# Router preparation moved ahead of the output projection, zero matmuls in the router's waits, and the first gather in two parts

## The chip, the cores and the metric

The kernel runs on one core of one Trainium2 chip. The metric is device microseconds (us) of one execution, from the first instruction to the end; lower is better. Engines are named as the profile names them: PE is the matmul engine, PEld its weight loads, DVE, ACT and POOL the elementwise engines, SP the engine that issues most transfers. The trailing q in SPq, ACTq or PEq means the engine's sequencer.

## What is computed

A batch of 1 with 256 tokens of 1024 features goes through one mixer block and then two decoder layers, all in float32. Each decoder layer has an attention half (three branches, gates, an output projection) and an experts' half. The experts' half is what the change touches:

```python
x = x + (gate1[:, None, :] * (merged.astype(x.dtype) @ w_o)).astype(x.dtype)
h2 = modulate(rms_norm_2(x, norm2_g), shift2, scale2)
y_moe = hier_moe(h2, w_router_group, b_router_group, w_router_expert, b_router_expert,
                 w_exp_gate, w_exp_up, w_exp_down)
x = x + (gate2[:, None, :] * y_moe).astype(x.dtype)
```

`hier_moe` scores 4 groups of 8 experts each, picks one group and two of its experts for each token, and adds up the chosen experts' outputs, weighted by both softmaxes. All 32 experts of a layer have three matrices of 2 MB.

## The kernel before, in words

**Weights.** Every weight matrix comes in chunks of 2 MB (128 partitions x 4096 columns). Each of the 32 experts has three chunks, `weg` (gate), `weu` (up) and `wed` (down). SP issues their transfers (line 429). One large tile, `memory`, holds everything; the class `Plan` gives each small tile and each chunk its columns from a dry run. A second tile is called `parts` while it holds split operands, and `spare` in the experts' half, where it takes two chunks. A transfer waits until the last reader of its columns is done, so when memory is full the next chunk waits for an expert's chunk to be used up. Eleven of a layer's 96 expert chunks are under way or there before the first expert runs; the twelfth (expert 3's `wed`) takes the columns of expert 0's `weg`.

**End of the attention half** (`front`, lines 1264 to 1297). `ma` holds the merged branches, split in high and low parts by ACT (L1284) and DVE (L1285); just before, DVE adds the last branch with L1281 (times the gate tile `g1`) and L1282 (the sum), in four pairs of feature tiles. The output projection `tm_out` then runs 96 matmuls of 512 columns into the PSUM banks `po`. `add_x` (DVE L600, ACT L592) adds them to x and takes its squares.

**Start of the experts' half** (`moe`, line 1705). The router's weights `wr` come by a POOL-issued transfer (line 396). Eight matmuls `shift @ wr` of 36 columns make the bias `br`, and eight DVE operations (L1735) make `wg_` = gain x `wr`. Four zero matmuls open the accumulators `acc`. `flip` (L631) transposes x, sixteen router matmuls of 36 columns follow, then some forty small DVE operations (L1746 to L1772), and four matmuls that count each token's place within its expert. `group(0)` gathers the tokens of experts 0 to 3:

```python
self.mm(p[:, i, :], self.x[:, t, j + i::8], S[:, t].rearrange("p e s -> p (e s)"), t == 0, t == 1)
```

Its 16 matmuls have x as the stationary operand, every eighth column of it, and the one-hot matrix `S` of 4 x 32 places as the moving one. DVE (L1824) and ACT (L1822) write the results to `XG`, in turn. Then comes `overflow`, a branch for experts with over 32 tokens that all engines take part in (not taken in this execution), then the transposes of `back(0)` (L1835), then expert 0: 64 matmuls on `weg`, 64 on `weu`, and so on. `XG[:, j, s]` with `s` the expert's 32 places is all that an expert reads of the group.

All matmuls through the helper `mm` show as line 505. Float32 matmuls show as two records each in the trace, transposes as one. Tile's scheduler, not the source alone, sets each engine's order; each engine then runs its own list strictly in order.

Of the kernel before, what the change touches and what calls it, by code (L numbers as in the profile page):

```python
# [21 lines left out]
# ---------------------------------------------------------------- host layout  # L22
# [5 lines left out]
def _chunk(w):  # L28
    """[K*128, N] -> [128, K*N], row d = 128*k + p at partition p."""
    kp, n = w.shape  # L30
    return w.reshape(kp // 128, 128, n).transpose(1, 0, 2).reshape(128, -1)
# [160 lines left out]
# ---------------------------------------------------------------- the kernel  # L192
class Act:
    """Activations, features on partitions: float32 and its exact two-part split."""
# [5 lines left out]
class Dry:  # L200
    """Stands for anything in the run that only plans the memory."""
# [22 lines left out]
class Plan:  # L224
    """Sizes and lifetimes of all tiles by a dry run, and from them each tile's place and each weight chunk's time to
    start: as early as there is room for it. Times count the steps of the program that take or free memory."""
# [19 lines left out]
    def place(self, first):  # L246
        """An address for every tile, from the bottom, and for every chunk while it is used, from the top: the large
        and long ones first, and before them those that found no room."""
# [28 lines left out]
    def early(self):  # L277
        """Every chunk in turn starts as early as some place is free for it, in the main part or, while that is open
        for chunks, in the other."""
# [26 lines left out]
class Memory:  # L306
    """Columns of one tile, given out and taken back in the order of the program; the waits follow from the data."""
# [6 lines left out]
    def step(self):  # L314
        """One step on; the chunks whose time has come start."""
# [6 lines left out]
    def new(self, *sh, p=128, part=0):  # L322
        """A tile of this shape on the first p partitions."""
# [22 lines left out]
    def chunk(self):  # L346
        """The next weight chunk's number."""
        self.step()
        if self.tiles is None:
            self.plan.chunks.append([Plan.CHUNK, self.now, None, 0])  # L350
        self.got += 1
        return self.got - 1
# [6 lines left out]
    def turn(self, key, *sh, bufs=2, p=128, part=0):  # L359
        """One of bufs tiles of this shape, by turns, until done()."""  # L360
# [11 lines left out]
class Kernel:  # L372
# [26 lines left out]
    def order(self):  # L399
        """The weight chunks in the order in which they are used."""  # L400
# [19 lines left out]
    def start(self, n, t):  # L420
# [4 lines left out]
        # an expert half's last chunk in parts, so that little work is left after the last of them  # L425
# [6 lines left out]
    def get(self, *key, k=8, hold=False):  # L432
        """The next weight chunk; it is there until the next call, or until drop()."""
# [20 lines left out]
    def run(self, plan, dry):  # L454
# [24 lines left out]
        # the last norm: all but the last quarter times its gain before the rows' rs is there  # L479
# [7 lines left out]
    # -- helpers  # L487
    def turn_part(self, spare):
        """The second part of the memory is for split operands, or it is spare and takes weight chunks."""
# [14 lines left out]
    def mm(self, out, lhsT, rhs, start, stop):  # L504
        self.nc.tensor.matmul(out, lhsT=lhsT, rhs=rhs, start=start, stop=stop)  # L505

    def psb(self, tag="sm", name="pst"):
        """A bank of PSUM."""
        return self.ps.tile([128, 512], F, tag=tag, bufs=BANKS[tag], name=name)

    def split(self, f, n=4):
        """f = hi + lo, both exact in the tensor engine's one-pass float32."""
# [6 lines left out]
    def unit(self, src, a, n=1024):  # L519
        """The split of 1024 weights a partition."""  # L520
# [6 lines left out]
    def mm3(self, jobs, left):  # L527
        """out += w.T @ a, or a.T @ w, for every out, w, a, start, stop, from the parts: those with the weights' high
        part first. The product of both low parts is below float32's own rounding."""
# [6 lines left out]
    def fm_pair(self, w, act, m, K=8):  # L536
        """Feature tiles m, m+1 of the projection of act, features on partitions."""
# [10 lines left out]
    def tm(self, w, act):  # L548
        """The projection of act, tokens on partitions: two banks of 128 tokens."""
# [8 lines left out]
    def tm_out(self, w, act, accs, first, last):  # L558
        """accs[t][h] += the projection of four feature tiles of act."""
# [9 lines left out]
    def rsqrt(self, out, in_, scale, eps, tmp):  # L569
        """out = (in_*scale + eps) ** -0.5 on small tiles."""  # L570
# [3 lines left out]
    def newton(self, out, v):  # L574
        """out = v ** -0.5: a first guess from the bits, then three Newton steps; v is overwritten."""
# [11 lines left out]
    def squares(self, t, h):  # L587
        """The mean square of half a row of x, into ss."""
# [5 lines left out]
    def add_x(self, accs, last=False):  # L594
        """x += accs, and its mean squares."""
# [9 lines left out]
    def last_gain(self):  # L605
        """The last norm's gain on every partition."""
# [18 lines left out]
    def flip(self, v, by8, use):  # L625
        """Two feature tiles of v's transpose at a time: use(k, their bank)."""
# [7 lines left out]
    def norm_T(self, gain, shift=None):  # L634
        """The split of x's rms-norm, transposed: uT[d, t] * gain[d] (+ shift[d])."""
# [28 lines left out]
    def weave(chain, dense):  # L664
        """Trace the steps of a chain with pieces of dense work between them."""
# [4 lines left out]
    # -- block 1  # L670
    def block1(self):
# [10 lines left out]
        def softplus(out, x, t):  # L682
            """out = max(x, 0) + log1p(exp(-|x|)); t: four scratch tiles."""
# [15 lines left out]
        # forget gates and time steps, heads on partitions  # L699
# [19 lines left out]
        # token-major dt, exp(cumsum), decay to the chunk's end  # L719
# [14 lines left out]
        def conv(p, raw, out, j, wn, bn, nt):  # L734
            """causal conv of width 4 of psum tile p along time."""
# [73 lines left out]
        def gates():  # L809
            """The z gates of LRU and SSD; SSD's norm, features on partitions."""  # L810
# [83 lines left out]
        def ssd():  # L894
            # B.C scores, masked to s <= l
# [7 lines left out]
            # tokens on partitions: x*dt and x*d, B of chunk 0  # L903
# [1089 lines left out]
```

## Time and profile before

| | |
|---|---|
| median of 3 runs | 1986.38 us (1982.15 to 1988.5) |
| span of the profiled execution | 1985.8 us |
| PE, DVE, ACT busy | 84%, 48%, 28% of the span |
| DMA, mean over the span | 295 GB/s of at most about 430 |
| mean granted PE clock | 0.915 |

The profiled execution's own time is not among the three; its span is 0.6 us under their median. Shares over the whole span say little here: the span has stretches bound by PE (attention halves) and stretches bound by transfers (experts' halves), and each has to be read by itself.

### The profile page before, as it was taken

The page shows a single profiled execution, that of the slowest core. Times are in us where ns is not written, and L with a number is a line of the kernel's source. Part 1 is how long each engine was busy: PE and PEld are TensorE (multiplying, and loading weights), DVE is VectorE, ACT ScalarE, POOL GpSimd, SP SyncE. Part 2 cuts the span into 40 slices and gives each one's busy share as a digit, 9 for nine tenths or more (in the row PEclk, how much of TensorE's full clock was granted, in tenths as well). Part 3 has the DMA queues.
Part 4 walks back from the last instruction along what each step waited for, and adds up shares of the span by engine and source line. Part 5 has one row for each costly group of instructions (what it writes and reads, how often), then busy time and mean ns, then how long its engine had stood idle before and what let it go on. Part 6 is the DMA issues. An engine that isn't in the chain of part 4 may idle for free. (4 is left out here: it accounts for less than half of the span.)

```text
span 1985.8 us, 42525 instructions
## 1 busy us (share of the span) xinstructions
PE 1659.6 (84%) x18982; PEld 1379.8 (69%) x18982; DVE 958.3 (48%) x2013; ACT 557.6 (28%) x856; POOL 76.6 (4%) x54
## 2 busy tenths in 40 slices
PE   6999999999999887776677599999988877667774
PEld 6877669788988765555455398889987765545553
DVE  7896556788438433222222456784376332222222
ACT  6835444524425300000000235244253100000001
POOL 0001000000004000000000000000040000000000
PEclk9999999999989899888888799999998998788888
DMA  8654563563325799999999953642258999999996
GB/s 344 236 193 155 201 262 131 212 251 132 128 100 234 291 426 426 426 427 425 427 427 426 399 221 133 259 161 105 109 188 324 391 426 425 427 426 426 426 426 252
DMA packets 43119, 586.13 MB, mean 295 GB/s; under 512 B 4816, under 2 KB 5456, under 8 KB 7984
## 3 DMA queue, kind: packets, MB, share of 16 engines
q1 hardware_dynamic: 41904, 579.72, 71.6%
q0 software_dynamic: 1024, 3.61, 0.5%
q8 instruction: 151, 2.47, 0.5%
q14 instruction: 40, 0.33, 0.0%
HBM read 582.26 MB, written 1.05 MB: 294 GB/s over the span
## 5 line engine op out<-in xcount | busy, mean ns | idle before, releaser
L505 PE MATMUL pst<-parts 128*128 128x256 f32 (+2 forms) x4344 | 636.6, 306 | 17.1 <-DVE parts L523 12.4
L505 PEld LDWEIGHTS pst<-parts 128*128 128x128 f32 (+1 forms) x4344 | 578.7, 197 | 65.8 <-issue 17.7
L505 PE MATMUL pst<-memory 128*32 128x256 f32 (+11 forms) x5152 | 519.7, 354 | 83.6 <-DMA memory<-in_wed_dram 43.5
L505 PEld LDWEIGHTS pst<-memory 128*32 128x32 f32 (+5 forms) x5152 | 373.7, 157 | 189.2 <-issue 115.9
L505 PE MATMUL pst<-memory,spare 128*32 128x128 f32 (+1 forms) x6848 | 266.1, 317 | 136.1 <-DMA memory<-in_weu_dram 77.4
L523 DVE TENSOR_TENSOR parts<-memory,parts 128x1024 fp32r<-128x1024 f32 (+1 forms) x233 | 296.7, 1276 | 156.6 <-ACT parts L522 147.6
L522 ACT ACTIVATE parts<-memory 128x1024 fp32r<-128x1024 f32 (+1 forms) x233 | 245.6, 1057 | 425.0 <-PE pst L505 348.1
L505 PEld LDWEIGHTS pst<-memory,spare 128*32 128x32 f32 (+1 forms) x6848 | 237.4, 129 | 178.8 <-issue 117.7
L1886 DVE TENSOR_TENSOR spare<-pst,memory 32x256 f32<-32x256 f32 x256 | 107.6, 420 | 172.0 <-PE pst L505 169.1
L1870 ACT ACTIVATE memory<-pst 128x128 f32<-128x128 f32 x64 | 25.2, 393 | 544.7 <-PE pst L505 525.9
L1872 DVE TENSOR_TENSOR memory<-memory,pst 128x128 f32<-128x128 f32 x64 | 24.0, 375 | 193.8 <-PE pst L505 193.7
L1871 DVE TENSOR_TENSOR memory<-memory,pst 128x128 f32<-128x128 f32 x64 | 24.2, 378 | 193.3 <-ACT memory L1870 193.3
L505 PE MATMUL po<-parts 128*128 128x512 f32 x384 | 89.6, 392 | 2.0 <-ACT parts L515 1.5
L505 PEld LDWEIGHTS po<-parts 128*128 128x128 f32 x384 | 71.5, 188 | 20.6 <-ACT parts L515 3.0
L1822 ACT ACTIVATE spare<-pst,memory,gain 128x128 f32<-128x128 f32 x64 | 29.3, 457 | 189.0 <-DVE spare L1824 189.0
L505 PE MATMUL pst<-spare 128*32 128x128 f32 x1408 | 51.0, 304 | 25.9 <-DMA spare<-in_weu_dram 12.9
L505 PEld LDWEIGHTS pst<-spare 128*32 128x32 f32 x1408 | 45.4, 123 | 32.8 <-issue 26.2
L505 PE MATMUL acc<-spare,memory 128*128 128x512 f32 x128 | 59.8, 610 | 9.2 <-DVE spare L1886 9.2
L1824 DVE TENSOR_SCALAR spare<-pst,gain,memory 128x128 f32<-128x128 f32 x64 | 26.2, 409 | 66.1 <-PE pst L505 56.7
L1291 POOL TENSOR_TENSOR memory<-memory 128x1024 f32<-128x1024 f32 x16 | 47.8, 3019 | 209.8 <-ACT memory L1145 209.8
L505 PEld LDWEIGHTS acc<-spare,memory 128*128 128x128 f32 x128 | 21.8, 189 | 38.1 <-DVE spare L1886 22.8
L505 PE MATMUL pst<-spare,memory 128*32 128x256 f32 x352 | 27.4, 459 | 14.5 <-DMA spare<-in_wed_dram 8.5
(381 smaller groups left out, 974.1 us busy)
## 6 DMA issues: line engine op xcount, KB each, us to landing
memory<-in_weg_dram SPq DMA_DIRECT2D x54, 2048.0 KB, 39.1
memory<-in_weu_dram SPq DMA_DIRECT2D x52, 2048.0 KB, 39.3
memory<-in_wed_dram SPq DMA_DIRECT2D x52, 2048.0 KB, 39.1
memory<-in_w_dram SPq DMA_DIRECT2D x33, 2048.0 KB, 8.6
memory<-in_ada_dram SPq DMA_DIRECT2D x24, 2048.0 KB, 7.6
memory<-in_wg_dram SPq DMA_DIRECT2D x12, 2048.0 KB, 8.2
spare<-in_weu_dram SPq DMA_DIRECT2D x12, 2048.0 KB, 39.1
spare<-in_wed_dram SPq DMA_DIRECT2D x10, 2048.0 KB, 40.5
```

Source lines behind the costliest of these rows:

```text
L505: self.nc.tensor.matmul(out, lhsT=lhsT, rhs=rhs, start=start, stop=stop)
L522: self.nc.scalar.activation(hi, src, AF.Copy)
L523: self.nc.vector.tensor_tensor(lo, src, hi.bitcast(F), op=OP.subtract)
L1291: nc.gpsimd.tensor_tensor(w[:, k], w[:, k], gb, op=OP.mult)
L1822: A.activation(XG[:, j + i, :], p[:, i, :], AF.Identity, scale=gain(j + i), bias=shift(j + i))
L1824: V.tensor_scalar(XG[:, j + i, :], p[:, i, :], gain(j + i), shift(j + i), op0=OP.mult, op1=OP.add)
L1870: A.activation(hf, pg, AF.Sigmoid)
L1871: V.tensor_tensor(hf, hf, pg, op=OP.mult)
L1872: V.tensor_tensor(hf, hf, pu, op=OP.mult)
L1886: V.tensor_tensor(Y[r, s], p[32 * c:32 * c + 32, 0:256], gb[32 * c:32 * c + 32, s], op=OP.mult)
```

## The change

The part of the router that needs no x (`gain`, `shift`, the load of `wr`, the gate rows `gb`, `br` and `wg_`) becomes a function `before_moe`, called ahead of the output projection's code. Twenty matmuls on a tile of zeros are added, which add nothing to `acc`. The first `group` is called with `ends` (0, 32, 128): its 16 matmuls and 8 copies are made for places 0 to 31 (expert 0), and again for places 32 to 127. `mm` becomes a property, so that matmuls show under their callers' lines. Removed comments and docstrings are left out here.

```diff
         mem.free(g1, mg, *ya.own)
+        self.before_moe(l)
         accs = [[self.psb("mm", name="po") for _ in range(2)] for _ in range(2)]
...
+    def before_moe(self, l):
+        nc, mem, V = self.nc, self.m, self.nc.vector
+        self.gain2, self.shift2 = gain, shift = self.gain_of(l, 1)
+        wrl = self.load(self.ap["wr"][l])
+        wr = wrl.rearrange("p (j n) -> p j n", j=8)
+        self.gb2 = self.gate_b(l, 1)
+        p = self.psb()
+        for j in range(8):
+            self.mm(p[:, 0:36], shift(j).to_broadcast([128, 128]), wr[:, j, :], j == 0, j == 7)
+        self.br, self.wg_ = mem.new(36), mem.new(8, 36)
+        V.tensor_tensor(self.br, p[:, 0:36], self.L(l, "br", 0, 36), op=OP.add)
+        for j in range(8):
+            V.tensor_scalar(self.wg_[:, j], wr[:, j], gain(j), None, op0=OP.mult)
+        mem.free(wrl)
...
+        def nothing(n, first=False):
+            for i in range(n):
+                self.mm(acc[i % 2][0], zero.to_broadcast([128, 128]), zero.to_broadcast([128, 512]), first, False)
+        nothing(2, True)
         for t in range(2):
-            for h in range(2):
-                self.mm(acc[t][h], zero.to_broadcast([128, 128]), zero.to_broadcast([128, 512]), True, False)
+            self.mm(acc[t][1], zero.to_broadcast([128, 128]), zero.to_broadcast([128, 512]), True, False)
+        nothing(6)
...
-        mem.free(xT)
+        mem.free(xT, wg_)
+        nothing(14)
...
-            for j in range(0, 8, 4):
-                p = self.psb("mm").rearrange("p (j s) -> p j s", j=4)
...
+            for s in (slice(*e) for e in zip(ends, ends[1:])):
+                for j in range(0, 8, 4):
+                    p = self.psb("mm").rearrange("p (j s) -> p j s", j=4)
+                    for i in range(4):
+                        for t in range(2):
+                            self.mm(p[:, i, s], self.x[:, t, j + i::8], S[:, t].rearrange("p e s -> p (e s)")[:, s], t == 0, t == 1)
...
-        nxt = group(0)
+        nxt = group(0, (0, 32, 128))
```

What the scheduler makes of it is the same in both layers. On PE, from the last matmuls before the output projection to the branch of `overflow`, the order before is this (`parts` are the split operands, `po` the projection's banks, `pst` any other bank, `zero` the tile of zeros):

```order
L505 MATMUL pst<-parts 128x256 x94
L505 MATMUL po<-parts 128x512 x96
L505 LDWEIGHTS zero
L505 MATMUL acc<-zero 128x512
L505 MATMUL pst<-memory 128x36 x8
L631 MATMUL pst<-memory 128x128 x16
L505 MATMUL pst<-memory,spare 128x36 x16
L505 MATMUL pst<-memory 128x64
L505 MATMUL pst<-memory 128x32 x3
L505 MATMUL pst<-memory 128x128 x16
L1903 TENSOR_LOAD memory
```

The eight `128x36` matmuls are `shift @ wr`, the sixteen are the router, the last sixteen are `group(0)`. After the change PE has this at the start of the output projection:

```order
L533 MATMUL pst<-parts 128x256 x8
L535 MATMUL pst<-parts 128x256 x4
L1716 MATMUL pst<-memory 128x36 x8
L533 MATMUL po<-parts 128x512 x8
L535 MATMUL po<-parts 128x512 x4
L533 MATMUL po<-parts 128x512 x8
L1748 LDWEIGHTS zero
L1748 MATMUL acc<-zero 128x512
```

The `shift @ wr` matmuls moved from behind all of the projection to right ahead of its first matmul, and one zero matmul into it. Between the projection and the gather PE has, from the sixth of the zero matmuls that follow the projection on:

```order
L1744 MATMUL acc<-zero 128x512
L632 MATMUL pst<-memory 128x128 x16
L1757 MATMUL pst<-memory,spare 128x36 x5
L1744 LDWEIGHTS zero
L1744 MATMUL acc<-zero 128x512
L1757 MATMUL pst<-memory,spare 128x36 x2
L1744 LDWEIGHTS zero
L1744 MATMUL acc<-zero 128x512
L1744 LDWEIGHTS zero
L1744 MATMUL acc<-zero 128x512
L1757 MATMUL pst<-memory,spare 128x36 x9
```

Six zero matmuls stand ahead of the transposes (L632), three among the router's (L1757), and eleven behind them. At the gather, down to the same branch, PE has:

```order
L1792 MATMUL pst<-memory 128x64
L1793 MATMUL pst<-memory 128x32
L1795 MATMUL pst<-memory 128x32
L1796 MATMUL pst<-memory 128x32
L1836 MATMUL pst<-memory 128x32 x2
L1836 MATMUL pst<-memory 128x96 x2
L1836 MATMUL pst<-memory 128x32 x14
L1836 MATMUL pst<-memory 128x96 x14
L1920 TENSOR_LOAD memory
```

Where 16 matmuls of 128 columns stood there are now 16 of 32 and 16 of 96 columns, all of them ahead of the branch, and so of expert 0. The gate rows `gb` stood ahead of the output projection before, too, and stay where they were. The orders on SP and POOL do not change at all. The plan changes little: the chunks take the columns that they took, and `wr` lies at columns 4368 to 4655 of `memory` (5392 to 5679 before). Both are columns of `g1`, so the load waits for DVE's L1282 that reads `g1` there: the fourth pair's (the last) before, the second pair's now.

## Rows read from the trace of the kernel before

**Rows 1.** Stretch, sum; busy time of PE, PEld, DVE, ACT, POOL; clock, DMA share, GB/s.

```profile
680.00:691.50 11.50, 9.07 (x110) 8.14 (x113) 3.42 (x12) 4.58 (x7) 0.00 (x0) 0.65 0.13 29
700.00:1100.00 400.00, 282.92 (x4906) 218.56 (x4910) 102.13 (x282) 26.89 (x64) 0.53 (x1) 0.89 1.01 426
1532.00:1542.00 10.00, 7.81 (x99) 7.44 (x101) 3.42 (x12) 3.95 (x7) 0.00 (x0) 0.84 0.04 11
1550.00:1960.00 410.00, 296.78 (x4998) 227.57 (x5002) 105.06 (x289) 28.07 (x66) 0.00 (x0) 0.86 1.01 426
```

**Rows 2.** The chain of waits, its last transfer: start us, us, what.

```profile
1943.36 26.05 DMA spare<-in_wed_dram
```

**Rows 3.** Timeline of SP, first chunk issued after layer 0's gap: start us, us.

```profile
690.38 0.34 SPq L429 DMA_DIRECT2D memory<-in_wed_dram  x1
```

**Rows 4.** Timeline of PE, layer 0: start us, us, instructions [idle before <-releaser].

```profile
640.16 21.95 PE L505 MATMUL po<-parts 128*128 128x512 f32 x96
662.18 1.87 PE L505 MATMUL pst<-memory 128*128 128x36 f32 x16
663.88 2.01 PE L631 MATMUL pst<-memory 128*128 128x128 f32 x16
665.73 3.75 PE L505 MATMUL pst<-memory,spare 128*128 128x36 f32 x32
673.60 1.89 PE L505 MATMUL pst<-memory 128*128 128x64 f32 x8 [4.12 <-DVE memory L1795]
675.78 7.88 PE L505 MATMUL pst<-memory 128*128 128x128 f32 x32 [0.29 <-DVE memory L1813]
686.09 0.66 PE L1835 MATMUL pst<-memory 128*128 128x128 f32 x2 [2.43 <-ACTq L1915]
686.68 6.40 PE L505 MATMUL pst<-memory,spare 128*32 128x128 f32 x128
```

**Rows 5.** Timeline of PE, layer 1.

```profile
1492.21 5.18 PE L505 MATMUL po<-parts 128*128 128x512 f32 x22
...
1527.83 7.88 PE L505 MATMUL pst<-memory 128*128 128x128 f32 x32 [0.29 <-DVE memory L1813]
1538.26 5.37 PE L505 MATMUL pst<-memory,spare 128*32 128x128 f32 x128
```

**Rows 6.** Timeline of DVE and POOL around the load of wr, both layers.

```profile
636.96 0.69 DVE L1282 TENSOR_TENSOR memory<-memory 128x512 f32<-128x512 f32 x1
642.91 0.69 DVE L1282 TENSOR_TENSOR memory<-memory 128x512 f32<-128x512 f32 x1
644.17 0.60 POOL L396 DMA_DIRECT2D memory<-in_wr_dram  x1 [24.31 <-DVE memory L1282]
649.09 1.29 DVE L1735 TENSOR_SCALAR memory<-memory,gain 128x36 f32<-128x36 f32 x8 [1.77 <-DMA memory<-in_wr_dram]
...
1489.00 0.69 DVE L1282 TENSOR_TENSOR memory<-memory 128x512 f32<-128x512 f32 x1
1496.19 0.59 POOL L396 DMA_DIRECT2D memory<-in_wr_dram  x1 [25.73 <-ACT parts L522]
1499.94 1.28 DVE L1735 TENSOR_SCALAR memory<-memory,gain 128x36 f32<-128x36 f32 x8 [0.57 <-DMA memory<-in_wr_dram]
```

**Rows 7.** Stretches within two gathers, PE alone: sum, busy (instructions), clock, DMA.

```profile
677.00:681.00 4.00, 4.00 (x19) 0.50 0.76 320
718.00:724.00 6.00, 6.00 (x27) 1.00 1.01 429
```

**Rows 8.** Timeline of PE, layer 0, the gate rows' matmuls.

```profile
626.05 1.50 PE L505 MATMUL pst<-memory 128*128 128x128 f32 x12
```

**Rows 9.** Two stretches after PE stood idle; columns as in rows 1.

```profile
613.80:620.60 6.80, 5.43 (x24) 5.20 (x24) 6.80 (x5) 1.90 (x3) 6.06 (x3) 0.50 0.01 1
685.50:692.20 6.70, 6.12 (x106) 5.31 (x110) 0.96 (x5) 3.49 (x5) 0.00 (x0) 0.50 0.21 43
```

**Rows 10.** Timeline of DVE, its four additions to x in layer 0.

```profile
660.56 2.65 DVE L600 TENSOR_TENSOR memory<-memory,po 128x512 f32<-128x512 f32 x4 [2.44 <-PE po L505]
```

## What is predicted

> **What bounds the kernel now.** I read the windows first, because shares over the whole span mix stretches with different limits. In the long middle of both experts' halves the DMA share is 1.01 at 426 GB/s while PE is busy 283 of 400 us in the one and 297 of 410 us in the other [rows 1]. There the transfers are the bound: an engine that is faster in these stretches gains nothing. But just ahead of each of them the transfers rest: their share is 0.13 from 680 to 691.5 us, and 0.04 from 1532 to 1542 us [rows 1]. Memory is full then. The chunk that ends the rest is expert 3's `wed`, which takes the columns of expert 0's `weg`, and SP issues it at 690.38 us [rows 3], that is after the first 64 of expert 0's 128 records, which begin at 686.68 us [rows 4]. From then on the chunks follow each other at full rate, and the chain of waits ends with one of them, from 1943.36 us on for 26.05 us [rows 2]. So each half lasts from this first release a fixed time. **What delays expert 0's first 64 records delays the end by as much, in each layer; what hurries them gains as much.** The sum is over the way from the output projection to there. PE walks it alone: projection, `shift @ wr`, `flip`, router, token count, gather, `back`, expert 0 [rows 4].
>
> **The start of the projection.** The order has `shift @ wr` right ahead of the projection's first matmul now, so all 96 of those queue behind the landing of `wr`, and behind them DVE, which adds `po` to x, and all the router. When does `wr` land? Before, in layer 0, the fourth pair's L1282 ends at 642.91 + 0.69 = 643.60, POOL issues the load at 644.17, which is 0.57 later, and `wr` is used at 649.09, 4.92 after the issue [rows 6]. Now the load waits for the second pair's, which ends at 636.96 + 0.69 = 637.65 [rows 6]; with the same 0.57 and 4.92 it lands at 643.14. The eight matmuls take 1.87 [rows 4], and the projection, which began at 640.16 [rows 4], begins at 645.01: **4.85 us later**. In layer 1 the same L1282 ends at 1489.00 + 0.69 = 1489.69; the transfer took 1499.94 − 1496.19 = 3.75 [rows 6], so I get 1489.69 + 0.57 + 3.75 + 1.87 = 1495.88 against 1492.21 [rows 5]: **3.67 later**. If layer 0's transfer took 3.75 as well, 1.17 fall away; if layer 1's took 4.92, 1.17 come on top.
>
> PE stands idle for about 643.14 − 640.16 = 3.0 us in layer 0 and 1.8 in layer 1. After a 2.43 us idle [rows 4] the granted clock read 0.50, which is 1.2 GHz, through the 6.7 us from 685.5 to 692.2 [rows 9]. In such a stretch 512 columns take longer: the projection's matmuls take 21.95 / 96 = 0.229 each [rows 4] and would take up to twice that. A stretch of 6.8 us [rows 9] would cost 3.4; half of a stretch, 1.7, is what I take for layer 0, because `shift @ wr` covers its start, and nothing for layer 1, whose idle is shorter than the 2.43. The bounds are 0 and 3.4 in each.
>
> [...]
>
> **From the projection to the gather.** One zero matmul in the projection costs what one of `po` costs, +0.2. Behind the projection `shift @ wr` (1.87) is gone, and six zeros stand there, 6 x 0.23 = 1.4. But `flip` waits for x as well, and DVE's additions end at 660.56 + 2.65 = 663.21 [rows 10], 1.1 after the projection's end at 640.16 + 21.95 = 662.11. The zeros end 1.4 behind it, at 663.5 on the old clock, where `flip` began at 663.88 [rows 4]: −0.4. The eleven zeros after the router take 2.5 and lie in PE's wait of 4.12 for DVE [rows 4], at no cost; without that cover they would cost the 2.5. The three among the router's matmuls have no cover: +0.7. The token count took 1.89 for 8 records, 0.236 each, twice the 0.117 of the router's (3.75 / 32) [rows 4]; if the zeros keep the clock at 2.4 GHz it takes 0.9 less, if not, the same. I take −0.5.
>
> **The gather.** It was 32 records in 7.88 us [rows 4], 0.246 each, and becomes 64, all ahead of the branch, and so of `back` and expert 0: the order shows that nothing of expert 0 starts after the first part. What does a record of 32 or 96 columns cost? If the moving columns set the pace, the two parts would share the old time. They don't: the router's matmuls move 36 columns in 0.117 [rows 4], and the gate rows' move 128 in 1.50 / 12 = 0.125 [rows 8]. What differs in the gather is its stationary operand, every eighth column of x, at twice that. Nor is it the clock: at 1.2 GHz 19 records took 4.00 us, at 2.4 GHz 27 took 6.00, with PE busy all the time in both [rows 7], that is 0.21 and 0.22. So I charge each strided load as before: 32 more, **+7.9 us in each layer**. The lower bound is a first part at the router's pace, 32 x 0.117 = 3.7; nothing or less would need cheaper strided loads, which is a rival below.
>
> [...]
>
> The eight more copies of DVE and ACT follow the matmuls part by part, and the last, of 96 places instead of 128, is no later behind its matmuls: 0. The idle of 2.43 around the branch [rows 4] stays. Expert 0's first 64 records took 690.38 − 686.68 = 3.70 at 1.2 GHz [rows 3, 4, 9]; at best 1.85 less, if the clock holds through the branch. As the idle ahead of them stays, I take 0.
>
> **Sum.** Layer 0: 4.85 + 0.2 + 1.7 − 0.4 + 0.7 − 0.5 + 7.9 = +14.45. Layer 1: 3.67 + 0.2 + 0 − 0.4 + 0.7 − 0.5 + 7.9 = +11.57. Together +26.0 on the profiled span of 1985.8, which lies 0.6 under the median of 1986.38: **2012 us**. With the bounds (both half-clock stretches absent or full, −1.7 or +5.1; first parts at 3.7, −8.4; token counts, −0.8 or +1.0; clock in expert 0, up to −3.3) the main case lies between about 2003 and 2021, since they don't fall together.
>
> **Rivals.**
> (a) *Time goes by columns and clock, the two parts share the old time.* For it: the gather ran mostly at 1.2 GHz. Against: 0.125 for contiguous loads of 128 columns and 0.21 to 0.22 for strided ones at both clocks [rows 7, 8]. The gather then costs between 0 and +3.7 in each layer, and the time is 2012 − 15.8 = 1996 to 2012 − 8.4 = 2004. Chance 0.09.
> (b) *The other side: the clock is the gather's pace.* The zeros hold PE at 2.4 GHz from the projection on; at 0.125 a record 64 records take 8.0 and the gather costs nothing, no stretch of the projection runs slow (−1.7), and expert 0 runs at full clock (−1.85 in each layer, since the release needs only half of its work). That gives 2012 − 15.8 − 1.7 − 3.7 = 1991, within 0.3% of before; it is decided at a record of 0.13 us and a clock of 1.00 in expert 0. Against it stand the 27 records in 6.00 us at full clock [rows 7]. [...] Chance 0.06.
> (c) *The transfers hide the delay.* The chunks would have to wait for something else at the gap's end. But they rest at a share of 0.13 and 0.04 [rows 1] with their queue full, and at 1.01 afterwards there is nothing to catch up with. It would give 1986; with a faster result from an overlap that I don't see, chance 0.03.
>
> **Chances.** Main case 0.82. About 0.3%, 6 us, is what a measurement of this kernel can tell from no change: slower 0.90 (main, (a)), same 0.07 ((b), part of (c)), faster 0.03. A range of 1998 to 2021 leaves out (b), (c) and a little at each end.
>
> **What the changed profile would show.** PE idle by 1.8 to 3.0 us right ahead of `shift @ wr`, put down to the transfer of `wr`; the projection starting some 4 to 5 us after the last branch's matmuls; a gather of 64 records in 15 to 16 us; SP's first chunk after the rest some 14 us later in layer 0 and 11 to 12 in layer 1, measured from the end of the last branch; and streams of the same length behind both. Wrong would be the forecast if `wr` landed ahead of the projection's turn (−1 to −3 a layer), if a record of 32 columns took well under 0.2, or if expert 0's first records came at full clock.

## The result, and the profile after

The changed kernel takes 2016.30 us (median of 4 runs, 2015.94 to 2016.67) against 1986.37 before: ratio 1.0154, 95% interval 1.014 to 1.0169, about 30 us slower. 2012 was forecast, with a range of 1998 to 2021.

The timeline of PE in the changed kernel, layer 0, from the last matmuls ahead of the projection to expert 0 (start us, us, instructions, in brackets the idle time before them and what ended it; `mm` now shows under its callers' lines):

```profile
635.62 0.64 PE L535 MATMUL pst<-parts 128*128 128x256 f32 x4
640.67 3.60 PE L1716 MATMUL pst<-memory 128*128 128x36 f32 x16 [4.42 <-DMA memory<-in_wr_dram]
644.08 3.66 PE L533 MATMUL po<-parts 128*128 128x512 f32 x8
...
669.13 1.95 PE L632 MATMUL pst<-memory 128*128 128x128 f32 x16
...
679.19 0.41 PE L1792 MATMUL pst<-memory 128*128 128x64 f32 x2 [1.72 <-DVE memory L1811]
...
680.86 15.54 PE L1836 MATMUL pst<-memory 128*128 128x32 f32 x64 [0.63 <-DVE memory L1829]
...
699.37 5.01 PE L1883 MATMUL pst<-memory,spare 128*32 128x128 f32 x128
```

Against [rows 4] two things stand out: PE idle for 4.42 us ahead of `shift @ wr`, ended by the transfer of `wr`, and a gather of 64 records in 15.54 us where 32 took 7.88. Layer 1 shows both again:

```profile
1508.34 3.60 PE L1716 MATMUL pst<-memory 128*128 128x36 f32 x16 [4.70 <-DMA memory<-in_wr_dram]
1511.74 3.36 PE L533 MATMUL po<-parts 128*128 128x512 f32 x8
...
1548.25 15.55 PE L1836 MATMUL pst<-memory 128*128 128x32 f32 x64 [0.63 <-DVE memory L1829]
...
1566.49 4.94 PE L1883 MATMUL pst<-memory,spare 128*32 128x128 f32 x128
```

The timeline of SP gives the first chunk after the rest in both layers, which answers to [rows 3]:

```profile
702.70 0.34 SPq L429 DMA_DIRECT2D memory<-in_wed_dram  x1
...
1569.76 0.34 SPq L429 DMA_DIRECT2D memory<-in_wed_dram  x1
```

The windows show PE's granted clock as a share of full speed (the number behind PE's busy time and, in brackets, the count of records that lie in the window, those that only reach into it included) around the projection's start and in the gather:

```profile
640.60:644.00 3.40, 3.33 (x16) 0.51 0.69 289
644.00:648.00 4.00, 4.00 (x12) 0.56 0.53 147
648.00:652.00 4.00, 4.00 (x18) 1.00 0.89 377
680.80:681.80 1.00, 0.94 (x4) 0.91 1.04 442
681.80:683.00 1.20, 1.20 (x7) 0.50 1.02 437
684.00:697.00 13.00, 12.41 (x52) 0.50 0.17 71
```

After the idle time PE ran at a clock of 0.51 and 0.56 until about 648. The prediction and the expectations write the clock in GHz, which no run shows; what is measured is this share. Behind the zero matmuls the clock read 1.00 at the token count (679 to 680.8 us; 0.50 before, from 673.6 to 675.6), but about a microsecond into the gather it fell to 0.50, with PE never idle since the gather's start.

**Where the time went.** Two executions differ by some us long before the change begins: the profiled one of the changed kernel reaches the end of the last branch's matmuls at 636.26 us, that of before at 640.33, 4.07 later, and most of that was there at 186 us. The executions of before in this study spread over 1981 to 1992 us (a single slow one of 3323, at a mean granted clock of 0.49, is left out). So the stages are compared from that point on, in each layer for itself. The table gives how much later (+) than before each stage begins in layer 0 / layer 1, worked out as the difference of PE's start times (SP's in the last row) less the difference at the end of the last branch's matmuls (before: 640.33 and 1492.37; changed: 636.26 and 1503.64). The other columns belong to the experiments below.

| stage begins | changed | e1 move only | e2 split only | e3 zeros only | e5 `wr` early | e6 other order |
|---|---|---|---|---|---|---|
| projection | +7.99 / +8.26 | +8.19 / +8.59 | 0 / 0 | 0 / 0 | +1.48 / +1.48 | 0 / 0 |
| projection ends | +9.93 / +9.92 | +10.06 / +10.78 | 0 / 0 | 0 / 0 | +2.04 / +2.05 | 0 / 0 |
| `flip` | +9.32 / +9.32 | +8.36 / +9.09 | 0 / 0 | +1.32 / +1.31 | +1.44 / +1.45 | 0 / 0 |
| token count | +9.66 / +9.66 | +9.03 / +9.77 | 0 / 0 | +1.73 / +1.73 | +1.78 / +1.79 | -0.15 / -0.15 |
| gather | +9.15 / +9.15 | +9.02 / +9.76 | 0 / 0 | +1.23 / +1.23 | +1.28 / +1.29 | -0.15 / -0.14 |
| gather ends | +16.82 / +16.82 | +9.02 / +9.77 | +7.65 / +7.64 | +1.22 / +1.23 | +8.94 / +8.95 | -2.29 / -2.38 |
| expert 0 | +16.76 / +16.96 | +8.77 / +9.77 | +7.59 / +7.83 | +1.22 / +1.48 | +8.88 / +9.08 | -2.53 / -2.39 |
| first chunk issued | +16.39 / +16.98 | +8.35 / +9.23 | +7.59 / +8.28 | +1.22 / +1.49 | +8.88 / +9.54 | -4.22 / -3.45 |

For the changed kernel: −4.07 ahead of the change, +16.39 in layer 0, −1.05 between the layers, +16.98 in layer 1 and +0.15 behind it make +28.4, the difference of the two spans (2014.2 and 1985.8). From layer 1's first chunk to the end the profiles of all twelve kernels take 443.5 to 445.6 us, although that chunk starts anywhere from 1515 to 1570: a delay there does come out at the end. From layer 0's first chunk to layer 1's last branch the seven kernels that keep before's order of features take 797.6 to 804.0, so there the −1.05 is within what executions differ by.

The stages add up to +33.4 in the changed kernel, while the medians differ by 29.9; in e5 they add up to +18.4, and the medians differ by 14.3. What makes up for it lies outside these stages. It is no larger than the differences between executions, but whether some of it belongs to the change is not shown.

### The profile page after: what moved, and what is told of

Its sections match the earlier page's. It is cut to its first block, busy times and chain, and to the rows that moved or that the text cites. A ratio compares the mean times of both kernels' runs of the same rounds, so it can differ in the third digit from the quotient of the medians.

```text
span 2014.2 us, 42747 instructions
## 1 busy us (share of the span) xinstructions
PE 1675.3 (83%) x19078; PEld 1393.1 (69%) x19086; DVE 960.0 (48%) x2021; ACT 560.5 (28%) x864; POOL 76.8 (4%) x54
## 3 DMA queue, kind: packets, MB, share of 16 engines
HBM read 582.26 MB, written 1.05 MB: 290 GB/s over the span
## 5 line engine op out<-in xcount | busy, mean ns | idle before, releaser
L533 PE MATMUL pst<-parts 128*128 128x256 f32 (+2 forms) x2896 | 458.6, 307 | 4.7 <-DVE parts L657 3.6
L533 PEld LDWEIGHTS pst<-parts 128*128 128x128 f32 (+1 forms) x2896 | 397.3, 198 | 43.3 <-issue 16.0
L1883 PE MATMUL pst<-memory,spare 128*32 128x128 f32 x6784 | 256.0, 313 | 149.1 <-DMA memory<-in_weu_dram 82.9
L1883 PEld LDWEIGHTS pst<-memory,spare 128*32 128x32 f32 x6784 | 227.1, 127 | 190.4 <-issue 130.1
L535 PE MATMUL pst<-parts 128*128 128x256 f32 (+2 forms) x1448 | 238.7, 302 | 11.4 <-DVE parts L524 11.4
L1899 PE MATMUL pst<-memory 128*32 128x256 f32 x1696 | 123.4, 435 | 65.9 <-DMA memory<-in_wed_dram 46.3
L1836 PE MATMUL pst<-memory 128*128 128x128 f32 (+2 forms) x576 | 141.5, 413 | 1.3 <-DVE memory L1829 1.3
L1836 PEld LDWEIGHTS pst<-memory 128*128 128x128 f32 x576 | 138.4, 335 | 5.2 <-issue 3.8
L1899 PEld LDWEIGHTS pst<-memory 128*32 128x32 f32 x1696 | 61.8, 121 | 111.2 <-issue 71.7
L1839 ACT ACTIVATE spare<-pst,memory,gain 128x128 f32<-128x128 f32 (+2 forms) x72 | 31.9, 445 | 203.5 <-DVE spare L1841 203.3
L1841 DVE TENSOR_SCALAR spare<-pst,gain,memory 128x128 f32<-128x128 f32 (+2 forms) x72 | 28.2, 394 | 82.0 <-PE pst L1836 72.3
L533 PEld LDWEIGHTS po<-parts 128*128 128x128 f32 x256 | 49.4, 196 | 16.2 <-ACT parts L516 3.0
```

Source lines behind the costliest of these rows:

```text
L533: self.mm(out, *((w[0], a[n]) if left else (a[n], w[0])), start and n == 0, False)
L535: self.mm(out, *((w[1], a[0]) if left else (a[0], w[1])), False, stop)
L1836: self.mm(p[:, i, s], self.x[:, t, j + i::8], S[:, t].rearrange("p e s -> p (e s)")[:, s], t == 0, t == 1)
L1839: A.activation(XG[:, j + i, s], p[:, i, s], AF.Identity, scale=gain(j + i), bias=shift(j + i))
L1841: V.tensor_scalar(XG[:, j + i, s], p[:, i, s], gain(j + i), shift(j + i), op0=OP.mult, op1=OP.add)
L1883: self.mm(ps[-1][32 * c:32 * c + 32, :], XG[:, j, s], w[:, j, 128 * c:128 * c + 128], j == 0, j == 7)
```

## Experiments

Each kernel was run in several rounds beside the kernel before, whose median was 1984.66 beside e1 to e4, 1985.35 beside e5 to e8 and 1985.91 beside e9 and e10.

**e1: the move alone.** The changed kernel without its extra zeros and with one gather.

```diff
-        nothing(6)
...
-        nothing(14)
...
-        nxt = group(0, (0, 32, 128))
+        nxt = group(0)
```

> The change with its twenty extra zero matmuls and its split gather taken back: only the router's preparation stands ahead of the output projection. Theory (each part costs its own time on PE's way to expert 0): the changed kernel's profile has the projection start 8.0 and 8.25 us later, its first matmuls at half clock for 1.9 us more, and 0.6 us back behind it, so +9 to +9.5 in each layer, 2004 to 2006. Rival (the move is free or is caught up, and the gather costs all of the 30 us): 1986 to 1988.

2001.59 us, ratio 1.0093 (1.0077 to 1.0108): 16.9 us for the move alone, 8.35 and 9.23 in the two layers. That is below the theory's 2004 to 2006; of the difference 1 us is the expert's first records, which took 0.4 and 0.5 less. The rival (1986 to 1988) falls. PE waits for `wr` for 4.62 us here, and `shift @ wr` runs as slowly as in the changed kernel:

```profile
639.45 3.60 PE L1716 MATMUL pst<-memory 128*128 128x36 f32 x16 [4.62 <-DMA memory<-in_wr_dram]
642.85 3.56 PE L533 MATMUL po<-parts 128*128 128x512 f32 x8
```

**e2: the split alone.** Before, with the changed kernel's `group` and:

```diff
-        nxt = group(0)
+        nxt = group(0, (0, 32, 128))
```

> The kernel before with the first gather in two parts and nothing else. Theory (each of the 32 more strided weight loads costs 0.24 us, whatever its moving columns): the gather takes 15.5 us for 7.9, +7.7 in each layer, 2002. Rival one (time goes with the moving columns, both parts share the old time): 1986 to 1994. Rival two (the clock sets the pace, and without zero matmuls it is low): more than 8 us in each layer, above 2003.

2001.06 us, ratio 1.008 (1.0062 to 1.0098): +16.4. The gather took 15.53 us for 64 records, 0.243 each, with 32 and 96 moving columns as with 128:

```profile
678.80 15.53 PE L505 MATMUL pst<-memory 128*128 128x32 f32 x64 [0.29 <-DVE memory L1813]
```

The theory holds to 0.1 us a layer in the gather and both rivals fall: without any zero matmul ahead of it the gather takes what it takes with them.

**e3: the zeros alone.** Before, with the changed kernel's `nothing` and its calls.

```diff
+        nothing(2, True)
         for t in range(2):
-            for h in range(2):
-                self.mm(acc[t][h], zero.to_broadcast([128, 128]), zero.to_broadcast([128, 512]), True, False)
+            self.mm(acc[t][1], zero.to_broadcast([128, 128]), zero.to_broadcast([128, 512]), True, False)
+        nothing(6)
...
+        nothing(14)
```

> The kernel before with the twenty zero matmuls and nothing else. Theory (they cost where nothing covers them, and give back only the token count's half clock): six ahead of shift at wr +1.4, three in the router +0.7, eleven hidden, token count -0.5 to -0.9: +1.2 to +1.6 in each layer, 1989. Rival (they keep the clock up through the gather and expert 0): gather unchanged, expert 0's first 64 records 1.4 to 1.8 us shorter in each layer, 1983 to 1986.

1987.97 us, ratio 1.0013 (0.9999 to 1.0028): +3.3, not told from nothing by the times, but by the stages: +1.22 and +1.49. PE's timeline around the router, and its windows in the gather:

```profile
655.87 1.70 PE L505 MATMUL acc<-zero 128*128 128x512 bf16 x7
657.41 1.87 PE L505 MATMUL pst<-memory 128*128 128x36 f32 x16
...
669.24 1.05 PE L505 MATMUL pst<-memory 128*128 128x64 f32 x8 [1.72 <-DVE memory L1802]
670.92 7.87 PE L505 MATMUL pst<-memory 128*128 128x128 f32 x32 [0.63 <-DVE memory L1820]
```

```profile
671.00:672.00 1.00, 1.00 (x5) 1.00 0.99 426
672.00:673.00 1.00, 1.00 (x6) 1.00 0.99 426
673.00:674.00 1.00, 1.00 (x6) 0.50 0.96 410
674.00:676.00 2.00, 2.00 (x10) 0.50 0.18 74
```

The token count is faster at a clock of 1.00 (669 to 671 us), as forecast: 1.05 us for the 1.89 that it took at 0.50 before [rows 4]. The gather is not: 5 to 6 records fall into each microsecond at either clock, and 7.87 us is what it took without zeros. Expert 0 gains nothing, since the clock has fallen long before it (0.50 from 681 to 685 us, over its first records). The rival falls at both places. The six zeros cost 1.3 here, where `shift @ wr` still stands behind the projection; in the changed kernel they stand in `flip`'s wait for DVE, at no cost. That is why the three parts add up to 36.2 us in the table's last row, and the whole change to 33.4.

**e4: adjoining columns by a copy.** Before, with ACT copying x in PE's wait behind the router, so that the first gather loads 128 adjoining columns.

```diff
+        xc = [mem.new(2, 4, 128, part=1), mem.new(2, 4, 128, part=0)]
+        for n in range(2):
+            for t in range(2):
+                A.activation(xc[n][:, t], self.x[:, t].rearrange("p (f j) -> p j f", j=8)[:, 4 * n:4 * n + 4], AF.Copy)
...
-                        self.mm(p[:, i, :], self.x[:, t, j + i::8], S[:, t].rearrange("p e s -> p (e s)"), t == 0, t == 1)
+                        self.mm(p[:, i, :], (xc[(j + i) // 4][:, t, (j + i) % 4] if g == 0 else self.x[:, t, j + i::8]), S[:, t].rearrange("p e s -> p (e s)"), t == 0, t == 1)
```

> The kernel before, with ACT copying x into a tile in which each feature group's columns lie side by side, in PE's wait after the router; the first gather (one part) takes its stationary operand from there. Theory (the stride of the stationary operand sets the gather's pace): 32 records at 0.125 us are 4.0 us for 7.9, -3.9 in each layer, 1978 to 1979. Rival (the clock sets it): at half clock still 0.24 a record, 1986.

1991.00 us, ratio 1.0037 (1.0023 to 1.0052): slower, so both expectations miss. The gather did get shorter, 6.1 us, but not 4:

```profile
673.91 3.75 PE L505 MATMUL pst<-memory,spare 128*128 128x128 f32 x16 [0.29 <-DVE memory L1817]
677.45 2.57 PE L505 MATMUL pst<-memory 128*128 128x128 f32 x16
```

```profile
674.00:675.50 1.50, 1.50 (x7) 0.50 0.00 0
...
679.00:680.00 1.00, 1.00 (x10) 1.00 0.00 0
```

At a clock of 0.50 an adjoining load with its matmul takes 0.234 us (3.75 for 16), about as much as a strided one (0.243 in e2); at 1.00 10 records fall into a microsecond. So clock and stride each cost a factor of about two, and they don't add up: whole gathers at 1.00 give 0.12 adjoining and 0.246 strided (3.84 and 7.88 for 32, under e8). What was gained went again: ACT's copies delayed the `Exp` that the router's weights wait for (PE's wait for DVE was 5.75 instead of 4.12), and the first chunk was issued 2.5 us later in layer 0 and 3.9 in layer 1 although expert 0 began 0.1 earlier. It was not PE that SP waited for there. Half of the copy lies in columns that an earlier chunk, expert 3's `weg`, takes, so SP could issue that one only at the gather's end, 43.3 us behind the last branch's matmuls instead of 29.9 in both layers (680.10 and 670.26 in layer 0). Behind it SP came to `overflow`'s branch 7.4 us later than before, and by the time SP had left it, at 688.9, PE was through all of expert 0's first 128 records (687.96). The first chunk followed at 689.37 with no further wait for PE. So this run's time does not price the stride: the copy put SP on the path to the first chunk in PE's place.

**e5: the whole change, with `wr` in time.**

```diff
             mem.done("bsg")
+            self.wrl = self.load(self.ap["wr"][l])
             ys["res"] = self.gate_b(l, 0)
...
-        wrl = self.load(self.ap["wr"][l])
+        wrl = self.wrl
```

> The whole change, but the transfer of wr is called before the last gate tile is made, so that its columns are free some 20 us earlier; the shift at wr matmuls stay ahead of the output projection. Theory (what the move costs is the wait for wr and the half clock that follows it, 9.3 us in each layer, not the place of the matmuls): both fall away, flip starts as early as DVE's additions let it, 9 to 10 us less in each layer than the changed kernel, 1996 to 1998. Rival (the place costs: the matmuls ahead of the projection hold it up whatever wr does): not below 2010.

1999.62 us, ratio 1.0069 (1.0056 to 1.0083) to before, 15.7 us of the 29.9 gone (by the stages 15.0 of 33.4): short of the 18 to 20 expected, but far under the rival's 2010. PE doesn't stop ahead of the projection:

```profile
636.76 0.64 PE L535 MATMUL pst<-parts 128*128 128x256 f32 x4
637.24 1.65 PE L1717 MATMUL pst<-memory 128*128 128x36 f32 x14
638.71 2.09 PE L533 MATMUL po<-parts 128*128 128x512 f32 x8
```

What is left of the move is what the matmuls take themselves, 1.48, and two zeros inside the projection; I had counted those as covered.

**e6: another order of features.** Instead of a copy, feature 128 k + p at partition p (8 p + k before), in the host's layout of `weg`, `weu`, `wr` and the second norm's gain, and in the device's columns of shift and scale.

```diff
-        a[n] = g(m).reshape(2, 32, 128, 4096)
+        a[n] = g(m).reshape(2, 32, 8, 128, 512).transpose(0, 1, 3, 2, 4).reshape(2, 32, 128, 4096) if n != "wed" else g(m).reshape(2, 32, 128, 4096)
...
-            if v in (3, 4):
+            if False:
...
-                        self.mm(p[:, i, :], self.x[:, t, j + i::8], S[:, t].rearrange("p e s -> p (e s)"), t == 0, t == 1)
+                        self.mm(p[:, i, :], self.x[:, t, (j + i) * 128:(j + i + 1) * 128], S[:, t].rearrange("p e s -> p (e s)"), t == 0, t == 1)
```

> The kernel before with another order of features in the experts' half (feature 128 k + p instead of 8 p + k at partition p, in the host's layout of weg, weu, wr, the second norm's gain and the shift's and scale's columns), so that the first gather and all later ones load 128 adjoining columns of x; nothing else. Theory (a strided load takes 0.22 to 0.24 us at both clocks, an adjoining one 0.23 at 1.2 GHz and 0.12 at 2.4): the first gather runs mostly at 1.2 GHz as in the run with the copy, 6 us for 7.9, -1.8 in each layer, 1981 where before gives 1985. Rival (stride alone): 4 us, -3.9 in each layer, 1977.

1961.47 us, ratio 0.9873 (0.9859 to 0.9888): 23.9 us faster than before, far more than either expectation. At the experts' start it gives 4.22 and 3.45, of which the gather has 2.1 and 2.2 (5.74 us, mostly at a clock of 0.50, as the first theory says) and expert 0's first records 1.7 and 1.1, at a clock that was back at the gather's end:

```profile
665.65 5.74 PE L505 MATMUL pst<-memory 128*128 128x128 f32 x32 [0.29 <-DVE memory L1813]
```

```profile
668.60:669.60 1.00, 1.00 (x6) 0.50 1.13 475
669.60:670.60 1.00, 1.00 (x11) 0.95 0.49 188
...
674.20:676.20 2.00, 2.00 (x77) 1.00 0.01 4
```

The other 16 us lie outside the experts' start; e9 asks where.

**e7: the same with the fourteen zeros** in and behind the router, as e3 has them.

```diff
         mem.free(xT)
+        nothing(14)
```

> The same with the fourteen zero matmuls in and after the router, none ahead of it. Theory: the zeros keep the granted clock at 2.4 GHz up to the gather, where adjoining loads can use it: token count -0.5, router +0.4 to +0.7, gather 4 us for 7.9; -3.7 to -4 in each layer, 1977. Rival (zeros don't help the gather): 1982, as without them plus 0.3.

1960.82 us, ratio 0.9879 (0.9864 to 0.9893): no difference from e6. The token count gained its 0.5 and the gather took 5.45 instead of 5.74; the clock read 1.00 ahead of the gather, 0.81 in its first microsecond and 0.50 in the next two. Both expected times were reckoned without the 16 us found with e6; of the theory, the 4 us falls, since the zeros bring the clock to the gather and don't hold it there.

**e8: the whole change in the other order of features**, the edits of e6 on the changed kernel, in its gather:

```diff
-                            self.mm(p[:, i, s], self.x[:, t, j + i::8], S[:, t].rearrange("p e s -> p (e s)")[:, s], t == 0, t == 1)
+                            self.mm(p[:, i, s], self.x[:, t, (j + i) * 128:(j + i + 1) * 128], S[:, t].rearrange("p e s -> p (e s)")[:, s], t == 0, t == 1)
```

> The whole change with the other order of features. Theory (the second part costs 32 more loads, now of adjoining columns): the gather of 64 records takes 7.7 to 8 us at 2.4 GHz instead of 15.5, 7.6 less in each layer, 2001; up to 12 us if the clock falls on the way, 2009. Rival (doubled instructions cost as such): 15.5, 2016.

1997.16 us, ratio 1.006 (1.0047 to 1.0073). The gather took 12.24 us, mostly at a clock of 0.50:

```profile
675.80 12.24 PE L1836 MATMUL pst<-memory 128*128 128x32 f32 x64 [0.63 <-DVE memory L1829]
```

```profile
676.80:677.80 1.00, 1.00 (x7) 0.50 1.03 442
...
682.00:685.00 3.00, 3.00 (x16) 0.50 0.02 8
```

For the gather that is the upper end of what the theory allowed (the time is below both expectations, because the 16 us found with e6 are in it). To e6 the change costs 35.7 us, more than the 29.9 that it costs to before: the second part lengthens the stretch of the gather in which the clock read 0.50, from 4 us in e6 (665.6 to 669.6) to at least 8.2 here (676.8 to 685). The next gather, in one part, ran at a clock of 1.00 from end to end in both kernels and shows the stride alone, first in the changed kernel, then here:

```profile
725.27 7.88 PE L1836 MATMUL pst<-memory 128*128 128x128 f32 x32
```

```profile
720.83 3.84 PE L1836 MATMUL pst<-memory 128*128 128x128 f32 x32
```

**e9: the shift's and scale's old matmuls put back** into e6, as work that nobody reads.

```diff
+                if v in (3, 4):
+                    o = slice(64 * h, 64 * h + 64)
+                    for j in range(8):
+                        self.mm(q[o, 8 + j:9 + j], r[:, j::8], one, True, True)
```

> The kernel before with the other order of features, and with the eight strided matmuls of 64 columns that made a shift's or scale's columns before put back as work whose result nobody reads (beside the four that make them now). Theory (of the 24 us that the other order gave, 16 come from these matmuls, half as many and unstrided, 1.9 us for each of the eight parts, and 7.7 from the experts' start): 1977 to 1983, and from the projection to the first chunk the same 3.5 to 4.2 us less in each layer. Rival (the 16 come from the experts' own matmuls or transfers in the new layout): 1962.

1992.22 us, ratio 1.0031 (1.0016 to 1.0046): 31 us more than e6, twice what was expected. The groups of matmuls of one column (line, shapes, count, busy us and mean ns, idle before), of before:

```profile
L505 PE MATMUL pst<-memory 128*128 128x1 f32 x128 | 16.6, 251 | 2.3 <-DVE memory L1100 2.1
L505 PE MATMUL pst<-memory 128*64 128x1 f32 x128 | 16.6, 259 | 2.9 <-DVE memory L1100 2.6 <-DVE memory L1215 0.3
```

of e6, where the second group has gone over into the first with half its number:

```profile
L505 PE MATMUL pst<-memory 128*128 128x1 f32 x192 | 24.0, 246 | 5.0 <-DVE memory L1100 4.6 <-DVE memory L1215 0.3
```

and of e9, which has both:

```profile
L505 PE MATMUL pst<-memory 128*128 128x1 f32 x192 | 23.8, 245 | 5.2 <-DVE memory L1100 4.7 <-DVE memory L1219 0.3
L505 PE MATMUL pst<-memory 128*64 128x1 f32 x128 | 16.6, 260 | 0.0
```

Their own 16.6 us are half of the 31. The windows around three of the eight parts point to the rest, of before, of e6 and of e9:

```profile
210.00:250.00 40.00, 40.00 (x216) 0.91 0.51 180
```

```profile
205.00:240.00 35.00, 35.00 (x202) 1.00 0.63 229
```

```profile
210.00:250.00 40.00, 40.00 (x185) 0.74 0.43 158
```

PE is busy without a gap in all three, and the lower the granted clock, the fewer records fall into a microsecond: 5.8 at 1.00, 5.4 at 0.91, 4.6 at 0.74. One execution of each is not enough, though. In e2, whose order here is that of before, the same stretch read:

```profile
205.00:240.00 35.00, 35.00 (x166) 0.73 0.44 161
```

Over 205 to 250 us the clock was 1.00 in all four kernels with four such matmuls in a part (e6, e7, e8, e10), 0.77 in e2 and 0.92 to 0.96 in the other six with eight, and 0.77 in e9 with twelve. From 1150 to 1300, around layer 1's four parts, it was 1.00, 0.95 to 0.97 and 0.94. So with eight the clock read lower than with four in every profile taken; that it reads lower still with twelve shows in layer 1 alone, and by little. The rival falls, since e9 keeps the new layout. That exactly the 16 us of e6 come from there is likely and not shown, because each part has twelve such matmuls in e9, eight in before and four in e6.

**e10: the other order of features with the move done without its wait**, one gather, no added zeros: the edits of e1, e5 and e6 on the changed kernel.

```diff
-        wrl = self.load(self.ap["wr"][l])
+        wrl = self.wrl
...
-        nothing(14)
...
-        nxt = group(0, (0, 32, 128))
+        nxt = group(0)
```

> The other order of features, with the router's preparation ahead of the projection and wr loaded early, one gather, no added zeros. Theory (nothing waits for wr, and of shift at wr's 1.9 us behind the projection only 0.5 were on the path, since flip waits for DVE's additions; ahead of it they cost 1.5): level with the other order alone to 1.5 us slower in each layer, 1961 to 1964. Rival (the preparation behind the projection costs its 1.9 us): 1958.

1965.11 us, ratio 0.99 (0.988 to 0.9919), 3.6 slower than e6: 1.1 above the theory's 1961 to 1964. `flip` begins 0.1 later than before, so what the move gives back behind the projection it takes ahead of it. The gather took 6.57 us for 5.74 in e6, and expert 0's first records 3.56 for 2.01: the clock came back almost 2 us later within the gather, and it read 0.50 to 0.70 while those records ran, against 1.00 in e6. The fastest kernel of the study remains e6, with e7 level, 24 us under before and 55 under the changed kernel.

## Why the prediction held, point by point

**The bound** held: layer 1's delay at the first chunk is its delay at the end, to 0.15 us, and layer 0's to the 1.05 by which executions differ anyway. That PE walks the way alone held for this change; e4 shows that SP can take its place.

**The gather** held. +7.9 a layer was forecast from strided loads at 0.246 us; e2 gives +7.65 and +7.64, 0.243 a record. Rivals (a) and (b) fall with e2 and e3. The 0.21 and 0.22 read from [rows 7] are too low, since these counts take in records that only reach into the window; whole gathers give 0.246 at a clock of 1.00 (7.88 for 32, under e8) and 0.243 at 0.50 (e2), so the conclusion stands. One reading behind it was too simple: that the clock has no part. It has none for strided loads, but adjoining ones are faster than these only at a clock of 1.00 (0.12 in e8 against 0.246; at 0.50 0.234 in e4 against 0.243). Why a strided load takes twice as long at 1.00 is not shown.

**The projection's start** was mis-sized. It was forecast 4.85 and 3.67 later; it was 7.99 and 8.26. The step that failed is the transfer of `wr`, priced at 4.92 and 3.75 us from its old place [rows 6]. POOL issued it when forecast, 0.58 after the second pair's L1283 (L1282 in before):

```profile
632.90 0.68 DVE L1283 TENSOR_TENSOR memory<-memory 128x512 f32<-128x512 f32 x1
```

```profile
634.16 0.59 POOL L396 DMA_DIRECT2D memory<-in_wr_dram  x1 [18.37 <-ACT parts L523]
```

but it took 6.4 us in layer 0 and 6.7 in layer 1, beyond the 4.92 that was allowed for as the longest. The earlier place lies in a stretch where the transfers of chunks fill the DMA engines, and the trace of before could have told it. On its clock the transfer was forecast for 638.2 to 643.1, and its windows read there:

```profile
634.00:640.00 6.00, 6.00 (x52) 1.00 1.00 429
640.60:644.00 3.40, 3.40 (x16) 1.00 1.02 434
```

Over the kernels of this study the same 144 KB took, from issue to landing, 2.4 and 2.6 us where the DMA share of the next 3.7 us was 0.14 (e5 and e10, layer 0), 3.2 to 3.8 where it was 0.74 to 0.83 (seven places), 4.9 to 5.1 at 0.90 to 0.93 (five), and 6.4 to 7.0 at 0.99 to 1.02 (six). In between the order is looser: 4.5 at 0.70, and 5.4 to 5.8 at 0.86 to 0.91 (three). No run changed the load alone, so this is a comparison of places.

**The half clock behind the wait** was forecast at 1.7 and 0. The idle was 4.4 and 4.7 us, not 3.0 and 1.8, and both layers paid, first of all in `shift @ wr`, which was to cover the start of the slow stretch and was not priced at half clock itself: `shift @ wr` took until 3.41 and 3.40 us after its start for 1.87, and the projection 23.89 and 23.61 for 21.95. That is 1.5 + 1.9 and 1.5 + 1.7 (0.2 to 0.3 of it the zero inside the projection), near the upper bound of 3.4 that was kept for it. In e5, without the idle, the projection took 22.51, two zeros included.

**The small terms.** `flip` −0.6 (forecast −0.4), the zeros in the router +0.34 (+0.7), the eleven behind it nothing (PE's wait until the token count 4.13, as before), the token count −0.51 (−0.5), copies and branch −0.06 and +0.14 (0), expert 0's first records −0.37 and +0.02 (0; the clock had fallen before them).

**The sum.** The terms came to +14.45 and +11.57 and were +16.39 and +16.98, 7.4 us more: 9.2 more up to the projection's end, all from `wr` and the clock behind it, and 1.9 less in the other terms. 5 us of that are hidden in the difference of the two profiled executions, most of which was there before the change's first instruction. So 2012 stood nearer to 2016.3 than its terms earned, which, as far as the runs tell, is luck.

**The signs named beforehand.** The gather of 15 to 16 us and the wait put down to `wr` came. The wait was longer than 1.8 to 3.0, the projection began 7.8 and 8.1 us after the last branch's matmuls instead of 4 to 5, and the first chunk came 16.4 and 17.0 later instead of 14 and 11 to 12. None of the signs of being wrong appeared.

## What to carry to other kernels

Price a moved transfer by the load of its new place, which the trace of before shows, and not by its old duration; then ask what stands behind its first reader in that engine's queue. Cutting a batch of small matmuls by their moving columns doubles the stationary loads, and where those set the pace, it doubles the time (the gather's 7.88 us became 15.53 in e2). When a kernel gathers every eighth column, look first at whether the layout of the weights can make the columns adjoin: here that was worth 24 us, with no instruction added, 7.7 of them between the projection and the first chunk, most of the others probably from halving the matmuls of one column that the old layout needed. A copy that makes the columns adjoin needs memory of its own: ask which transfer then waits for it (e4).

## What the runs showed of the hardware

- The granted clock fell while PE was busy without a gap: to 0.50, 0.6 to 2.1 us after the start of layer 0's gathers that had begun at 1.00 (changed kernel, e3, e7, e8; PE had been idle for 1.72 and 0.63 us just ahead of them), and below 1.00 in stretches of 35 and 40 us without any idle time in which matmuls of one column stood among others (mean clock 0.91 before, 0.73 in e2, 0.74 in e9, against 1.00 in e6). By these rows PE's busy share alone doesn't tell its clock.
- A stationary load of 128 columns with its matmul took 0.243 us strided at a clock of 0.50 (e2) and 0.246 at 1.00 (changed kernel), 0.234 adjoining at 0.50 (e4), and 0.12 adjoining at 1.00 (e8).
- The same 144 KB transfer took 2.4 to 7.0 us, the longer the higher the DMA share in its first 3.7 us (0.14 to 1.02), with some disorder between 0.70 and 0.91.
